# A two-layer decoder trunk: adaLN weights summed along rows on VectorE instead of multiplied on TensorE

## The chip, the cores and the metric

One NeuronCore of a Trainium2 chip runs the whole program. The metric is the device time of one execution in microseconds (us), as the median of several runs. TensorE is called PE in the rows (PEld is its weight load), VectorE DVE, ScalarE ACT, GpSimd POOL and SyncE SP.

## What is computed

Two layers work on x, which has 256 tokens of 2048 channels. The one vector c (2048 long) gives a shift, a scale and a gate for each channel of each layer:

```python
for li in range(DEPTH):                                   # DEPTH = 2
    mod = jax.nn.silu(c) @ w_ada[li] + b_ada[li]          # (2048) @ (2048, 6144)
    shift, scale, gate = jnp.split(mod, 3, axis=-1)
    h = rmsnorm(x, g_pre[li]) * (1.0 + scale) + shift
    p = split_columns(h @ w_in[li])                       # q, k, v, latents, indexer, gate columns
    ...                                                   # four token mixers A, B, C, D, 4 heads each
    mixed = concat(out_a, out_b, out_c, out_d) * silu(p["gate"])
    y = mixed @ w_out[li]
    x = x + gate * rmsnorm(y, g_post[li])
```

The line with `mod` is a matrix of 2048 by 6144 against a single vector, 50 MB of weights a layer that are each used once. The change is to this line alone. The large products (`w_in`, `w_out`) have 256 rows.

## The kernel before

**Large products.** Weights come as raw tiles of 128 x 1024 floats (512 KB, eight buffers called `raw`, DMAs issued by SP). ScalarE rounds each to `whi` (L279), VectorE subtracts to get `wlo` (L280), three buffers of each; then TensorE takes three products (`mm3`, L299 to L301: high by high, high by low, low by high). One raw tile is worth 24 products of 256 columns or 12 of 512. So each raw tile costs all three engines something, and each can run ahead of TensorE by as many tiles as there are buffers.

**Activations.** `modulated` (L433 to L436) scales x by `gain`, adds `shift` and splits the result into `act_hi` and `act_lo`. It needs the shift and gain of its 256 channels (one `k2` of eight), so it waits for their part of the adaLN product. `PHASES` says which k2 are taken together: layer 0 takes k2 0, then 1, then 2 and 3, and so on, layer 1 takes four at a time.

**adaLN.** The first two units of layer 0 (k2 0 and 1, `opening`) are 16 raw tiles that go through TensorE at once. The other 11 units, of 16 raw tiles each (layer 0: three of shift and scale, two of gate; layer 1: four and two), are a list of chunks that `Ada.run` hands out beside the large products: after every second raw tile `due` grows by a `PACE` of the stage, and for each whole 1 in it a chunk is issued. Most chunks are multiplied on VectorE by silu(c) (one value a partition, the input channel) and added to `ada_acc` (L131, L133). `PE_TILES` says how many of 16 go through TensorE instead (L141, `columns`: four products with 32 columns of weights each). At a unit's end `ada_acc` is summed over partitions by four more products with `ones` (L141), the result is in PSUM and is transposed (L162) into `shift` and `gain`, or gets bias and `g_post` (L182, L183) and goes to DRAM as `row` (L185), from where it is read back as a broadcast (L919). `until` issues what is left before a phase needs it; these all go through TensorE, as do five more at the start of layer 1 (`BOUND`).

**Order.** A scheduler orders each engine's instructions by priorities and its own estimate of time; engines take them strictly in that order. Between the layers the last tile of `w_out` is normed, x is updated (L960), squared and turned, and only then can layer 1 start.

## Time and profile before

| what | value |
|---|---|
| median of 3 runs | 1130.66 us (1130.19 to 1130.88) |
| the profiled execution | 1129.64 us |
| its span, first to last instruction | 1127.5 us |
| busy: TensorE | 1094.2 us, 97% |
| busy: VectorE | 848.9 us, 75% |
| busy: ScalarE | 553.9 us, 49% |
| read from HBM | 289.21 MB |

The span is what the rows below divide up; 2.1 us of the profiled execution lie around it. A share over the whole span mixes stages with different limits. In the span, 0 to 43 us is the opening, 43 to 60 the second phase's start, 60 to 490 the rest of layer 0 up to `w_out`, 490 to 571 `w_out` of layer 0, 571 to 592 the boundary, 592 to 900 the part of layer 1 that still has adaLN chunks, and 900 to 1127 the rest.

### The profile page before, as it was taken

The numbers are of one execution on the slowest core, as the hardware profiler recorded it, in microseconds if no ns is written. First come the engines' busy times: TensorE is split into PE (matmuls) and PEld (weight loads), VectorE is DVE, ScalarE is ACT, GpSimd is POOL, SyncE is SP. The second block draws the span as 40 slices with busy tenths as digits, with TensorE's granted clock in tenths as the row PEclk, the third lists the DMA queues.
The fourth block names the chain that finished last, engine by engine and source line by source line (L and its number), as shares of the span: only waits on it lengthen the run. The fifth ranks groups of instructions, "written<-read, shape, count | busy, mean of one in ns | idle before, by whom it ended". The sixth has DMA issues, their size and how long they took to land.

```text
span 1127.5 us, 19886 instructions
## 1 busy us (share of the span) xinstructions
PE 1094.2 (97%) x7818; PEld 991.5 (88%) x7818; DVE 848.9 (75%) x1221; ACT 553.9 (49%) x925; POOL 45.8 (4%) x57
## 2 busy tenths in 40 slices
PE   4899999999999999999989999999999999999996
PEld 3798989989899999988759999998899799999885
DVE  4587898889999978886549777899997555556454
ACT  3455344344464746754435445554644386645451
POOL 1000000000010100000000000100031000000000
PEclk9999999999999999999989999999999999999998
DMA  9997989868758888786869997977587654458642
GB/s 361 367 369 268 370 292 343 320 227 299 254 168 279 296 271 299 251 269 232 274 227 406 333 337 251 318 246 239 166 303 264 226 165 171 135 183 256 193 151 74
DMA packets 83101, 294.74 MB, mean 261 GB/s; under 512 B 9416, under 2 KB 9712, under 8 KB 83008
## 3 DMA queue, kind: packets, MB, share of 16 engines
q1 hardware_dynamic: 81216, 288.33, 73.5%
q0 software_dynamic: 1648, 5.09, 1.3%
q8 instruction: 61, 1.00, 0.4%
q14 instruction: 32, 0.26, 0.1%
q10 hardware_dynamic: 144, 0.07, 0.0%
HBM read 289.21 MB, written 4.23 MB: 260 GB/s over the span
## 4 chain that ended last, share of the span: by engine, by line
PE 89%; DVE 4%; DMA 3%; issue 1%; ACT 1%; SPq 0%; POOL 0%; DVEq 0%; POOLq 0%; ACTq 0%
PE main L299 26%; PE main L301 26%; PE main L300 26%; DMA raw<-in_w_ada_dram 3%; PE ada_ps L141 2%; DVE wlo L280 1%; PE att L491 1%; PE att L651 1%; PE att L508 1%; PE att L463 1%; DVE ada_acc L133 1%; DVE big L960 1%; ACT main L378 1%; PE att L616 0%; PE att L719 0%
## 5 line engine op out<-in xcount | busy, mean ns | idle before, releaser
L279 ACT CAST whi<-raw 128x1024 fp32r<-128x1024 f32 (+2 forms) x340 | 348.9, 1027 | 400.4 <-PE main L300 205.4
L280 DVE TENSOR_TENSOR wlo<-raw,whi 128x1024 fp32r<-128x1024 f32 (+2 forms) x340 | 404.7, 1195 | 155.4 <-ACT whi L279 153.8
L299 PE MATMUL main<-act_hi,whi 128*128 128x256 f32 x1568 | 440.0, 283 | 1.6 <-DVE lat_acc L369 1.6
L300 PE MATMUL main<-act_lo,whi 128*128 128x256 f32 x1568 | 441.0, 283 | 0.0
L301 PE MATMUL main<-act_hi,wlo 128*128 128x256 f32 x1568 | 433.1, 284 | 0.9 <-DVE wlo L280 0.8
L299 PEld LDWEIGHTS main<-act_hi,whi 128*128 128x128 f32 x1568 | 295.7, 189 | 5.7 <-issue 3.9
L300 PEld LDWEIGHTS main<-act_lo,whi 128*128 128x128 f32 x1568 | 295.6, 189 | 3.1 <-issue 2.0
L301 PEld LDWEIGHTS main<-act_hi,wlo 128*128 128x128 f32 x1568 | 290.7, 189 | 5.6 <-DVE wlo L280 2.3
L133 DVE SCALAR_TENSOR_TENSOR ada_acc<-raw,sc,ada_acc 128x1024 f32<-128x1024 f32 x144 | 184.7, 1282 | 35.8 <-DMA raw<-in_w_ada_dram 34.9
L300 PE MATMUL main<-wlo,act_hi 128*128 128x512 f32 (+2 forms) x552 | 209.3, 381 | 0.4 <-DVE wlo L280 0.3
L301 PE MATMUL main<-whi,act_lo 128*128 128x512 f32 (+2 forms) x552 | 206.7, 379 | 0.0
L299 PE MATMUL main<-whi,act_hi 128*128 128x512 f32 (+2 forms) x552 | 191.5, 381 | 4.8 <-ACT act_hi L435 4.8
L299 PEld LDWEIGHTS main<-whi,act_hi 128*128 128x128 f32 x552 | 103.3, 190 | 26.0 <-ACT act_hi L435 6.1
L300 PEld LDWEIGHTS main<-wlo,act_hi 128*128 128x128 f32 x552 | 104.5, 190 | 23.2 <-issue 2.7
L301 PEld LDWEIGHTS main<-whi,act_lo 128*128 128x128 f32 x552 | 104.4, 190 | 19.4
L141 PE MATMUL ada_ps<-raw,crep 128*32 128x128 f32 (+1 forms) x424 | 26.9, 381 | 12.8 <-DVE on L391 12.7
L100 POOL TENSOR_TENSOR rstd<-ms,mhalf 128x1 f32<-128x1 f32 (+1 forms) x12 | 8.9, 744 | 573.3 <-DVE ms L99 573.3
L141 PEld LDWEIGHTS ada_ps<-raw,crep 128*32 128x32 f32 x424 | 13.9, 131 | 20.5 <-DVE on L391 12.7
L455 ACT ACTIVATE lat_acc<-lat_acc,mx 128x256 f32<-128x256 f32 (+1 forms) x56 | 25.2, 452 | 8.9 <-DVE mx L453 8.9
L949 ACT ACTIVATE wk<-main 128x512 f32<-128x512 f32 x16 | 9.5, 594 | 31.4 <-PE main L301 31.4
L659 DVE SCALAR_TENSOR_TENSOR cbuf<-wk,wid,cbuf 128x128 f32<-128x128 f32 (+1 forms) x64 | 24.2, 412 | 0.1
L656 ACT ACTIVATE wk<-att 128x256 f32<-128x256 f32 (+1 forms) x32 | 15.2, 488 | 18.2 <-DVE cbuf L659 13.0
(201 smaller groups left out, 873.5 us busy)
## 6 DMA issues: line engine op xcount, KB each, us to landing
raw<-in_w_g_dram SPq DMA_DIRECT2D x240, 512.0 KB, 5.4
raw<-in_w_ada_dram SPq DMA_DIRECT2D x192, 512.0 KB, 5.4
raw<-in_w_out_dram SPq DMA_DIRECT2D x64, 512.0 KB, 4.6
raw<-in_w_g_dram SPq DMA_DIRECT2D x16, 400.0 KB, 5.9
raw<-in_w_g_dram SPq DMA_DIRECT2D x16, 384.0 KB, 4.1
raw<-in_w_uq_dram SPq DMA_DIRECT2D x6, 384.0 KB, 4.0
big<-in_xt_dram SPq DMA_DIRECT2D x4, 512.0 KB, 6.8
raw<-in_w_ukv_dram SPq DMA_DIRECT2D x4, 512.0 KB, 4.4
```

Source lines behind the costliest of these rows:

```text
L133: nc.vector.scalar_tensor_tensor(self.acc, w, sc[:, kt:kt + 1], self.acc, op0=ALU.mult, op1=ALU.add)
L141: nc.tensor.matmul(self.ps[32 * q:32 * q + 32, 0:n], lhs, w[:, n * q:n * (q + 1)], start=not self.started, stop=last, tile_position=(0, 32 ...
L279: nc.scalar.copy(hi, src)
L280: nc.vector.tensor_sub(lo, src, hi)
L299: nc.tensor.matmul(out, sh, mh, start=first, stop=False, **kw)
L300: nc.tensor.matmul(out, sh, ml, start=False, stop=False, **kw)
L301: nc.tensor.matmul(out, sl, mh, start=False, stop=last, **kw)
L378: nc.scalar.activation(jk, L.cols(t, 512 * h, 512), AF.Square, accum_out=ssp[:, h:h + 1])
L455: nc.scalar.activation(lg[:, i, :], lg[:, i, :], AF.Exp, bias=mx[:, i:i + 1], accum_out=sm[:, i:i + 1])
L463: nc.tensor.transpose(tp[:, b * P:(b + 1) * P], pr[:, b * P:(b + 1) * P], ident)
L656: nc.scalar.activation(rl[:, 0:2 * sw], dp[:, 0:2 * sw], AF.Relu)
L659: nc.vector.scalar_tensor_tensor(sc[t], rl[:, u * sw:(u + 1) * sw], wid[:, t, h:h + 1], sc[t], op0=ALU.mult, op1=ALU.add)
```

## The change

The chunks after the opening units are laid out the other way around: output channels on partitions, input channels along the row. A unit is now one k2 (256 channels of shift and of scale) or four columns of gates, with 8 chunks, so the number of raw tiles stays 176 beside the opening's 16. Each chunk is one VectorE instruction: the tile times 0.5 times a row of silu(c), summed along the row into one column of `part`. `make_row` fills that row for all partitions: a broadcast DMA of c (1 MB written to `scb`, on POOL's queue), four tanh on ScalarE and four instructions of 512 columns on VectorE. A unit ends with one addition of its parts and the two or three small instructions of 2 to 4 columns that the bias needs; L141 remains for the opening alone. The gate is now written to DRAM from a tile of 128 x 8 as 1024 single floats. The biases and `g_post` come with the small constants, so four DMAs of 256 KB go away. To make room, `crep` takes the place of `strip`, and the tile `on` has one buffer instead of two. Paces change, `PE_TILES` and `BOUND` go.

```diff
-PACE = {"phase1": 1.5, "phase": 1.7, "last": 1.25, "gate0": 0.25, "gate1": 1.75, "gate2": 1.75, "gate3": 1.5, "d": 1.0, "out": 0.5, "next": 1}
+PACE = {"open": 0, "phase1": 1.75, "phase": 1.7, "last": 1.25, "gate0": 0.5, "gate1": 1.75, "gate2": 1.75, "gate3": 1.75, "d": 1.0, "out": 1.0, "next": 1}
-PE_TILES = {"phase1": 0, "phase": 2, "last": 2, "gate0": 1, "gate1": 1, "gate2": 0, "gate3": 0, "d": 0, "out": 2, "next": 0}
-UPTO = [[None, None, (0, 1), (0, 2), (0, 3)], [None, (1, 3)]]
+UPTO = [[None, None, (0, 3), (0, 5), (0, 7)], [None, (1, 7)]]
...
+    scb = const.tile([P, D], F32, name="scb")
+    def make_row():
+        row = a["c_row"]
+        nc.gpsimd.dma_start(scb, bass.AP(tensor=row.tensor, offset=row.offset, ap=[[0, P], [1, D]]))
+        for q in range(4):
+            v = scb[:, 512 * q:512 * (q + 1)]
+            th = work.tile([P, 512], F32, name="wk")
+            nc.scalar.activation(th, v, AF.Tanh, scale=0.5)
+            nc.vector.scalar_tensor_tensor(v, th, 1.0, v, op0=ALU.add, op1=ALU.mult)
...
-            if on_pe:
-                self.columns(crep[:, kt, :], w, last and self.acc is None)
-            elif self.acc is None:
-                self.acc = lay.tile([P, 1024], F32, name="ada_acc")
-                with tc.issue_after(self.behind):
-                    nc.vector.tensor_scalar(self.acc, w, sc[:, kt:kt + 1], None, op0=ALU.mult)
-            else:
-                nc.vector.scalar_tensor_tensor(self.acc, w, sc[:, kt:kt + 1], self.acc, op0=ALU.mult, op1=ALU.add)
-            if last:
-                if self.acc is not None:
-                    self.columns(ones[:, 0:32], self.acc, True)
+            with tc.issue_after(self.behind):
+                nc.vector.scalar_tensor_tensor(w, w, 0.5, scb[:, 1024 * (n % 2):1024 * (n % 2 + 1)],
+                                               op0=ALU.mult, op1=ALU.mult, accum_out=self.part[:, n:n + 1])
+            if n == 7:
                 self.finish(layers[li], li, u)
...
         def finish(self, L, li, u):
+            v = small.tile([P, 4], F32, name="parts")
+            nc.vector.tensor_add(v, self.part[:, 0:8:2], self.part[:, 1:8:2])
+            if u < K2:
+                self.modulation(L, u, v[:, 0:2], v[:, 2:4])
...
+                gc = self.gate[:, 4 * j:4 * j + 4]
+                nc.vector.tensor_add(gc, v, L.par[:, c0:c0 + 4])
+                nc.vector.tensor_mul(gc, gc, L.par[:, c0 + 16:c0 + 20])
+                if j == 1:
+                    L.row[h] = row = dram.tile([8, P], F32, name=f"row{li}{h}")
+                    nc.gpsimd.dma_start(bass.AP(tensor=row.tensor, offset=row.offset, ap=[[1, P], [P, 8]]), self.gate)
...
         if li == 1:
-            ada.until(1, 1)
-            ada.step(BOUND, on_pe=True)
+            ada.until(1, 3)
```

On TensorE, in layer 0's second phase, before. The rows with `ada_ps` are adaLN (a chunk, then the sum over partitions with `ones`), the others `w_in` products:

```order
L299 MATMUL main<-whi,act_hi_278 128x512 x2
L141 MATMUL ada_ps<-raw,crep 32x256 x4
L141 MATMUL ada_ps<-ada_acc,ones 32x256 x2
L300 MATMUL main<-wlo,act_hi_278 128x512
L301 MATMUL main<-whi,act_lo_282 128x512
```

The same place now:

```order
L304 MATMUL main<-whi,act_hi_278 128x512 x2
L305 MATMUL main<-wlo,act_hi_278 128x512
L306 MATMUL main<-whi,act_lo_282 128x512
```

All such rows after the opening are gone from TensorE; nothing takes their place.

On VectorE, at the start of the second phase (about 43 us), before. `sml` are the small constants, `big_96` is x:

```order
L162 STREAM_TRANSPOSE wk<-ada_ps 128x128
L168 TENSOR_TENSOR shift<-wk,sml 128x2
L170 SCALAR_TENSOR_TENSOR gain<-wk,sml 128x2
L172 TENSOR_TENSOR gain<-gain,sml 128x2
L433 SCALAR_TENSOR_TENSOR wk<-big_96,gain,rrow 128x256 x2
L280 TENSOR_TENSOR wlo<-raw,whi 128x768
L436 SCALAR_TENSOR_TENSOR act_lo_282<-wk,shift,act_hi_278 128x256 x2
L131 TENSOR_SCALAR ada_acc<-raw,sc 128x1024
L133 SCALAR_TENSOR_TENSOR ada_acc<-raw,sc,ada_acc 128x1024 x2
L280 TENSOR_TENSOR wlo<-raw,whi 128x1024
```

The same place now:

```order
L161 STREAM_TRANSPOSE wk<-ada_ps 128x128
L118 SCALAR_TENSOR_TENSOR scb<-wk,scb 128x512
L171 TENSOR_TENSOR shift<-wk,sml 128x2
L173 SCALAR_TENSOR_TENSOR gain<-wk,sml 128x2
L118 SCALAR_TENSOR_TENSOR scb<-wk,scb 128x512
L175 TENSOR_TENSOR gain<-gain,sml 128x2
L118 SCALAR_TENSOR_TENSOR scb<-wk,scb 128x512
L438 SCALAR_TENSOR_TENSOR wk<-big_96,gain,rrow 128x256 x2
L285 TENSOR_TENSOR wlo<-raw,whi 128x768
L118 SCALAR_TENSOR_TENSOR scb<-wk,scb 128x512
L441 SCALAR_TENSOR_TENSOR act_lo_282<-wk,shift,act_hi_278 128x256 x2
L137 SCALAR_TENSOR_TENSOR raw,part<-raw,scb 128x1024 x3
```

Four instructions of `make_row` stand between the opening's last transpose and the first adaLN chunk.

On VectorE at the start of layer 1 (about 587 us), before; `att` holds x turned:

```order
L433 SCALAR_TENSOR_TENSOR wk<-att,gain,rrow 128x256 x6
L280 TENSOR_TENSOR wlo<-raw,whi 128x800
L436 SCALAR_TENSOR_TENSOR act_lo_6428<-wk,shift,act_hi_6424 128x256
L280 TENSOR_TENSOR wlo<-raw,whi 128x800
L436 SCALAR_TENSOR_TENSOR act_lo_6428<-wk,shift,act_hi_6424 128x256 x3
L131 TENSOR_SCALAR ada_acc<-raw,sc 128x1024
L436 SCALAR_TENSOR_TENSOR act_lo_6429<-wk,shift,act_hi_6425 128x256 x2
L433 SCALAR_TENSOR_TENSOR wk<-att,gain,rrow 128x256 x2
L280 TENSOR_TENSOR wlo<-raw,whi 128x768
```

The same place now:

```order
L438 SCALAR_TENSOR_TENSOR wk<-att,gain,rrow 128x256 x6
L441 SCALAR_TENSOR_TENSOR act_lo_6377<-wk,shift,act_hi_6373 128x256 x3
L438 SCALAR_TENSOR_TENSOR wk<-att,gain,rrow 128x256 x2
L441 SCALAR_TENSOR_TENSOR act_lo_6377<-wk,shift,act_hi_6373 128x256
L137 SCALAR_TENSOR_TENSOR raw,part<-raw,scb 128x1024 x3
L441 SCALAR_TENSOR_TENSOR act_lo_6378<-wk,shift,act_hi_6374 128x256 x4
L137 SCALAR_TENSOR_TENSOR raw,part<-raw,scb 128x1024 x2
L285 TENSOR_TENSOR wlo<-raw,whi 128x768
L285 TENSOR_TENSOR wlo<-raw,whi 128x800
```

The first three subtractions of layer 1 (800, 800 and 768 columns) have moved ahead of the boundary, behind those of `w_out`; five chunks now stand ahead of the fourth.

## Rows read from the trace of the kernel before

**Rows 1.** Page, chain that ended last, share of the span by engine

```profile
PE 89%; DVE 4%; DMA 3%; issue 1%; ACT 1%; SPq 0%; POOL 0%; DVEq 0%; POOLq 0%; ACTq 0%
```

**Rows 2.** Stretches: length, us of PE, PEld, DVE, ACT, POOL; clock; DMA share, GB/s

```profile
4.00:14.00 10.00, 1.17 (x20) 0.74 (x24) 5.63 (x14) 4.57 (x10) 0.00 (x0) 1.00 1.01 397
...
43.00:60.00 17.00, 13.31 (x90) 12.38 (x90) 16.82 (x26) 6.14 (x7) 0.57 (x1) 0.90 0.98 375
60.00:490.00 430.00, 429.30 (x3211) 397.30 (x3208) 377.20 (x550) 217.73 (x376) 18.50 (x22) 1.00 0.82 286
245.00:365.00 120.00, 120.00 (x900) 110.50 (x899) 114.79 (x205) 59.65 (x108) 5.99 (x9) 1.00 0.77 258
490.00:571.00 81.00, 81.00 (x361) 63.65 (x360) 46.07 (x44) 33.54 (x43) 0.00 (x0) 1.00 0.74 248
...
592.00:900.00 308.00, 307.94 (x2255) 286.50 (x2254) 254.06 (x374) 152.40 (x241) 18.00 (x15) 1.00 0.80 282
```

**Rows 3.** Waits, 60 to 490 us: waiter, releaser: total us, times, longest

```profile
DVE wlo L280 <- ACT whi L279: 29.8, 33, 2.5
DVE ada_acc L133 <- DMA raw<-in_w_ada_dram: 9.7, 6, 2.0
...
PE main L301 <- DVE wlo L280: 0.7, 2, 0.5
```

**Rows 4.** Stretches, line 141 alone: PE busy, PEld busy, clock, DMA

```profile
60.00:490.00 430.00, 9.79 (x100) 2.60 (x96) 1.00 0.82 286
490.00:571.00 81.00, 1.91 (x20) 0.46 (x20) 1.00 0.74 248
571.00:592.00 21.00, 8.97 (x100) 3.75 (x100) 0.85 0.73 254
592.00:900.00 308.00, 4.40 (x32) 1.02 (x32) 1.00 0.80 282
```

**Rows 5.** Timeline of PE around one adaLN sum: start, us, instruction

```profile
94.58 0.40 PE L301 MATMUL main<-whi,act_lo 128*128 128x512 f32 x1
94.91 0.63 PE L141 MATMUL ada_ps<-ada_acc,ones 128*32 128x256 f32 x4
95.46 0.73 PE L299 MATMUL main<-whi,act_hi 128*128 128x512 f32 x2
96.03 0.40 PE L300 MATMUL main<-wlo,act_hi 128*128 128x512 f32 x1
```

**Rows 6.** Groups by line: count, busy us, mean ns of one, idle before

```profile
L133 DVE SCALAR_TENSOR_TENSOR ada_acc<-raw,sc,ada_acc 128x1024 f32<-128x1024 f32 x144 | 184.7, 1282 | 35.8 <-DMA raw<-in_w_ada_dram 34.9
L455 ACT ACTIVATION_READ_ACCUMULATOR lat_acc<-lat_acc,mx 128x1 f32 x56 | 10.5, 187 | 0.0
L391 DVE TENSOR_TENSOR on<-on,wk 128x512 f32<-128x512 f32 x7 | 4.8, 691 | 1.3 <-ACT wk L389 0.9
L172 DVE TENSOR_TENSOR gain<-gain,sml 128x4 f32<-128x4 f32 (+1 forms) x9 | 1.4, 159 | 0.2
```

**Rows 7.** Stretches, tile ada_acc alone: PE, PEld and DVE busy

```profile
60.00:490.00 430.00, 5.62 (x48) 1.53 (x48) 105.42 (x85) 1.00 0.82 286
...
592.00:900.00 308.00, 4.40 (x32) 1.02 (x32) 73.85 (x59) 1.00 0.80 282
```

**Rows 8.** Timeline of the boundary, PE and DVE

```profile
587.08 4.50 PE L141 MATMUL ada_ps<-raw,crep 128*32 128x256 f32 x40
587.48 2.44 DVE L433 SCALAR_TENSOR_TENSOR wk<-att,gain,rrow 128x256 f32<-128x256 f32 x6 [0.42 <-ACT rrow L411]
591.50 1.02 PE L299 MATMUL main<-whi,act_hi 128*128 128x400 f32 x2
592.04 1.27 DVE L436 SCALAR_TENSOR_TENSOR act_lo<-wk,shift,act_hi 128x256 fp32r<-128x256 f32 x3
599.37 0.95 DVE L280 TENSOR_TENSOR wlo<-raw,whi 128x768 fp32r<-128x768 f32 x1
```

**Rows 9.** Page, DMA issues: count, KB each, median us to landing

```profile
strip<-line POOLq DMA_DIRECT2D x1, 1536.0 KB, 14.0
```

More of the change, by code (lines that the diff above doesn't have):

```diff
@@ L60 @@
 OWN3 = 1
-SM_PAR, SM_LAM, SM_END = 16, 128, 640
+UNITS_OF = 12
+SM_PAR, SM_LAM, SM_END = 16, 196, 708
+N_PAR = 90
 @with_exitstack
@@ L103, in trunk @@
     sc = const.tile([P, KT], F32, name="sc")
-    crep = const.tile([P, KT, 32], F32, name="crep")
+    crep = lay.tile([P, 12 * S], F32, name="strip")[:, 0:32 * KT].rearrange("p (k r) -> p k r", r=32)
     nc.scalar.activation(sc, c_sb, AF.Tanh, scale=0.5)
@@ L171, in to_columns @@
                                            op0=ALU.add, op1=ALU.add)
[L172 removed]
+            nc.vector.tensor_mul(g, g, L.par[:, 32 + 2 * k2:34 + 2 * k2])
         def finish(self, L, li, u):
[L175 to L185 removed]
+            v = small.tile([P, 4], F32, name="parts")
@@ L187, in stage @@
         def stage(self, name, unit):
-            self.pace, self.pe, self.unit = PACE[name], PE_TILES[name], unit
+            self.pace, self.unit = PACE[name], unit
         def add(self, li, u):
-            self.todo += [(li, u, n) for n in range(KT)]
+            self.todo += [(li, u, n) for n in range(8)]
         def run(self, pace):
@@ L196, in run @@
                 self.due -= 1
-                self.step(on_pe=(self.todo[0][2] + 1) * self.pe % 16 < self.pe)
+                self.chunk(*self.todo.pop(0))
         def until(self, li, u):
             while self.todo and self.todo[0][:2] <= (li, u):
-                self.step(on_pe=True)
+                self.chunk(*self.todo.pop(0))
             self.due = 0.0
-        def step(self, n=1, on_pe=False):
-            for _ in range(n):
-                if self.todo:
-                    self.chunk(*self.todo.pop(0), on_pe)
     ada = Ada()
@@ L248, in load_small @@
             nc.vector.tensor_scalar(L.gsub[:, j:j + 1], L.par[:, 53:54], (1.0 - lam_init) / (1 + j), None, op0=ALU.mult)
-    strip = const.tile([P, 12, S], F32, name="strip")
+    strip = None
     def make_strip():
+        nonlocal strip
+        strip = lay.tile([P, 12, S], F32, name="strip")
         hot = work.tile([P, 512], F32, name="wk")[0:32, 0:384]
@@ L383, in norm_rows_of_turned @@
     def norm_rows_of_turned(L):
-        acc = work.tile([P, 2, S], F32, name="on", bufs=2)
+        acc = work.tile([P, 2, S], F32, name="on", bufs=1)
         for k2 in range(K2):
@@ L694, in branch_d @@
         for t in range(T):
-            on = work.tile([P, 512], F32, name="on", bufs=2)
+            on = work.tile([P, 512], F32, name="on", bufs=1)
             ssq = small.tile([P, 4], F32, name="dss")
@@ L829, in layer @@
             if li == 0 and n < 2:
-                ada.stage("out", 0)
-                ada.pace = 0 if n == 0 else PACE["phase"]
-                ada.pe = PE_TILES["phase"]
+                ada.stage("phase" if n else "open", 0)
             else:
                 ada.stage(("last", "next")[li] if end else ("phase", "phase1")[li], UNIT["early"] if end and li == 0 else 0)
-            ada.limit = upto or (1, 5)
+            ada.limit = upto or (1, UNITS_OF)
             if li == 1 and n == 0:
@@ L861, in layer @@
                             next(units)
+                make_row()
                 continue
@@ L975, in trunk @@
     ada.pace = 0
-    for u in range(1, 4):
+    for u in range(2, K2):
         ada.add(0, u)
@@ L979, in trunk @@
         if li == 0:
-            for l, u in ((0, 4), (0, 5), *((1, u) for u in range(6))):
+            for l, u in (*((0, u) for u in range(K2, UNITS_OF)), *((1, u) for u in range(UNITS_OF))):
                 ada.add(l, u)
```

69 lines of the change are left out of this document (28 added, 41 removed).

## The prediction, made before the changed kernel was run

> **What bounds the kernel now.** I read the chain that ended last first: 89% of it is TensorE [rows 1]. Then the stretches [rows 2]: from 60 to 490 us TensorE is busy in 429.3 of 430 us, in `w_out` and in layer 1 all the time. So what leaves TensorE there is gained, unless another engine becomes late. VectorE is the only candidate: 377.2 of 430 us in layer 0, 114.79 of 120 (95.7%) between 245 and 365 us, and still no stall of TensorE there. Third, who waits [rows 3]: between 60 and 490 us TensorE waits 0.7 us for VectorE. VectorE's own largest wait, 29.8 us, is for ScalarE's `whi`, which comes late because its three buffers are full: real slack. Another 9.7 us are waits for the adaLN tiles themselves, which are no use to anyone. The kernel is bound by TensorE, with VectorE close behind it in layer 0.
>
> **What TensorE loses.** The rows of line 141 [rows 4] are its adaLN work: 9.79 us from 60 to 490, 1.91 in `w_out`, 8.97 at the boundary, 4.40 in layer 1. Busy time is not the price, since a switch of tile costs something on both sides. In the timeline [rows 5] a `ones` sum of two products of 0.63 us stands between main products that otherwise follow each other by 0.23 us (in `w_out` of 512 columns the same). From the start of L301 at 94.58 to that of L300 at 96.03 are 1.45 us, for three main products (0.69): the sum costs 0.76 us, 1.2 times its busy time. So 11.8 us go in layer 0, 2.3 in `w_out`, 5.3 in layer 1. The boundary I take below.
>
> **What VectorE gets.** The old multiply-add, with two float tiles read from SBUF, takes 1.282 us [rows 6]; the new one has the same size and two such inputs, so this is its price before the summing output. VectorE has no instruction of that kind in this kernel. ScalarE has: each of its summing instructions shows a second row that reads the sum, 0.187 us [rows 6]. I call this extra r, per chunk: 0 at one end (it may be hidden under the next start), 0.19 at the other; I take 0.1, the middle, since VectorE's own small instructions are shorter (0.159 us for four columns [rows 6], which overlap).
>
> The Trainium skill, page "VectorE: DVE Perf Modes", section "Two Vector instructions with no wait between them", says that an instruction that also writes out its accumulator is two instructions, the main one and an accumulator read. No run of before shows that on VectorE; the ScalarE row agrees in kind. By that rule r is above 0: at 0.19 the sum is that of rival 2 below, while at 0 it would be some 4 us under the forecast.
>
> In layer 0 from 60 us to `w_out` the new order has, by count, 97 chunks (105 up to the first `w_out` evacuation, less 8 in the second phase's start): 97 x 1.282 = 124.4 us for the 105.42 of before [rows 7]; 48 small instructions instead of 12, 36 x 0.159 = 5.7. Transposes and bias additions that go (some 3.5 us) offset the rest of the small stuff in part; I take them off: 377.2 + 19.0 + 5.7 - 3.5 = 398.4 us, and 97r on top: 398 to 417, 408 at r = 0.1. TensorE needs 430 - 11.8 = 418.2. So VectorE would be at 95.3% of the new length with r = 0, just what 245 to 365 us bears without a stall, at 97.6% with 0.1 and at 99.7% with 0.19. An engine that takes instructions in order, with waits for tiles between them, doesn't reach 100%. With 0.1 the length lies between TensorE's need, 418, and VectorE's work at that 95.7%, 408 / 0.957 = 426: I take 422.5, a gain of **7.5 us** instead of 11.8 (bounds 12 and a loss of 5).
>
> **The opening** pays for `make_row`. Its DMA writes 1 MB, stands third on POOL's queue and so runs with x and the first weights, where DMA is full at 397 GB/s (the 4 to 14 us row [rows 2]): 1.05 MB / 397 = **2.6 us** (bounds 0, if the opening waits for something else, and 2.6). Then, from 43 to 60 us, VectorE is busy 16.82 of 17 us while TensorE has gaps [rows 2]: here VectorE is the bound. The new order puts four instructions of 512 columns there, 4 x 0.69 = 2.8 us [rows 6], ahead of the first chunk; the first chunk of a unit was a cheaper form (some 0.5 us), and r counts six times (0.6): **3.9 us** (bounds 2.5, as the four tanh and part of this may fall into waits, and 6.5, as two more chunks come before the tenth split). ScalarE's four tanh lie beside it; its 6.14 of 17 us hide them. TensorE is full from 60 us on, so this delay stays to the end.
>
> **`w_out` and the rest of layer 0.** The pace there doubles, five chunks more: 46.07 + 5 x 1.4 = 53 of 79 us, hidden. The gain is 2.3 us.
>
> **The boundary.** At 587.08 us TensorE still has 4.50 us of adaLN work, and the first product of layer 1 follows at 591.50 [rows 8]. Nothing of it is left, and the first two splits lie ahead of the boundary, so that product could start some 1.5 us earlier. But VectorE's order now is: six scalings (2.44 us from 587.48), three `act_lo` (1.27), two scalings and one `act_lo` (1.2), three chunks (3.8), four `act_lo` (1.7), two chunks (2.6), and only then the fourth split: its start at 600.5 us against 599.37 for the fourth before [rows 8]. TensorE has three tiles' work for that time, 12 products of at most 0.23 us each [rows 5], 8 us, and runs out. I take **+1 us** (bounds -2 and +4). The granted clock of this stretch is 0.85 on average [rows 4], a mix of its two levels; I count neither loss nor gain of clock.
>
> **Layer 1, 592 to 900 us.** 62 chunks for 73.85 us of multiply-adds [rows 7]: 79.5, small instructions 3, less transposes: 254.06 + 5.6 + 6 = 266 of 303 us, 88%. TensorE's 5.3 us are gained but for 1 us of stalls where VectorE is dense (the attention stages): **4.3**.
>
> **At nothing.** The gate's row is written as 1024 single floats from POOL. The nearest row is `strip`, 1536 pieces in 14.0 us [rows 9]. Behind the last gate product some 27 (layer 0) and 47 (layer 1) splits of about 1.2 us stand in VectorE's order before the row is used, 30 us and more; without that cover it would cost some 15 us per layer. The four DMAs of 256 KB that go were off the path. `on` with one buffer makes ScalarE wait for four transposes between two halves of branch D; ScalarE is busy 217.7 of 430 us [rows 2], so nothing (up to 1 us a layer without that slack). `crep` in `strip`'s place is free long before `strip` is filled.
>
> **The sum.** +2.6 + 3.9 - 7.5 - 2.3 + 1.0 - 4.3 = -6.6 us against the profiled execution's 1129.64 (span 1127.5 and 2.14 around it): 1123.0. That execution lies 1.0 us under the median, so **1124 us** as a median, and 1117 to 1130 by the smaller bounds.
>
> **Rivals.**
> 1. *All of it is gained*: r near 0 and no stalls. +2.6 + 3.3 - 11.8 - 2.3 - 1.0 - 5.3 = -14.5: 1116 us (1110 to 1117). For it: 245 to 365 us runs at 95.7% without stalls, and the new paces put chunks where VectorE was idle. Against it: in-order waits and any r.
> 2. *VectorE becomes the bound of layer 0*: r = 0.19, 417 us of work at the 95.7%: 435.5 for the 430 of before, +5.5. With +2.6 + 4.4 for the opening, -1.5, +2.5 for the boundary (five chunks are 1 us longer) and -2.5: +11, 1142 us; 1131 to 1142 by how dense VectorE can run. It decides from r of about 0.11 (at 95.7%) to 0.19 (at 97.5%): there layer 0 gives less than the opening takes. For it: VectorE's 16.82 of 17 us at 43 to 60 with gaps on TensorE. Against it: TensorE's mere 0.7 us of waiting now.
> 3. *The change doesn't do what it says*, because another stall takes the place of the old work, so that the time stays: within 0.2%. The order shows the products gone, so this is only a balance of the terms above, 1130 us.
>
> **How the numbers follow.** Forecast 0.47, rival 1 0.23, rival 2 0.22, rival 3 0.08. A measurement of this kernel can tell about 0.2% (2.3 us) from no change: 1128.4 to 1132.9. Of the forecast's own range nearly all lies under 1128.4 (0.39), rival 1 wholly (0.23): faster 0.62. Same: 0.07 + 0.04 + 0.07 = 0.18; slower 0.20. The range reaches into rival 1 and half of rival 2: 1112 to 1137 leaves out about 1 in 10 at the top and some 0.07 below.
>
> **What would show it.** Line 141's successor has no TensorE row after 43 us. The new chunk's rows show 1.28 us, and whether a second row stands behind each: this decides between the rivals. TensorE's waits on VectorE between 60 and 490 us: under 1 us in rival 1, some 4 us here, over 15 in rival 2. Layer 0's `w_out` starts some 1 us earlier than now in my sum (6.5 lost, 7.5 gained). The first full stretch of TensorE starts 5 to 7 us later than 56 to 60. I'd be wrong if the opening hides the 1 MB, if the boundary stalls more than 4 us, or if DMA waits of chunks spread on the fuller VectorE.

## The result, and the profile after

The changed kernel takes **1179.79 us** (median of 4 runs, 1175.63 to 1181.93); the kernel before, beside it, 1130.77 (1130.19 to 1131.22). The ratio is 1.0429, 95% interval 1.0399 to 1.0459. It is slower by 49 us; the prediction said 1124 and at most 1137. The profiled execution has a span of 1180.2 us against 1127.5.

The page of the kernel after: the span, the busy times and the chain that ended last, to be held against [rows 1].

```profile
span 1180.2 us, 19623 instructions
...
PE 1098.7 (93%) x7562; PEld 1009.3 (86%) x7562; DVE 872.0 (74%) x1466; ACT 557.2 (47%) x929; POOL 38.7 (3%) x54
...
PE 67%; DMA 15%; DVE 12%; issue 3%; ACT 1%; SPq 0%; POOL 0%; DVEq 0%; POOLq 0%
```

TensorE's share of the chain falls from 89% to 67%; a load (DMA, 15%) and VectorE (12%) take its place. Over the span VectorE is no fuller than it was (74%, before 75%; 872 us of work, before 849): it is late, not overloaded. The groups by line show the new instruction, to be held against the first of [rows 6] (columns as there):

```profile
L137 DVE SCALAR_TENSOR_TENSOR raw<-raw,scb 128x1024 f32<-128x1024 f32 x176 | 214.3, 1223 | 99.8 <-DMA raw<-in_w_ada_dram 99.4
...
L137 DVE DVE_READ_ACCUMULATOR raw<-raw,scb 128x1 f32 x176 | 14.6, 83 | 0.0
```

A second row does stand behind each instruction, 83 ns long, but the instruction that follows starts together with it (both at 339.04 in the timeline below). So it takes no time of its own: where VectorE does not wait, 1.144 us pass from the start of a tile's instruction to the start of the next one (median of 162), and 1.197 us did for the old multiply-add (127). What is worse than before is the last number of the first row: VectorE stands still for 99.4 us in front of these instructions because the tile has not landed; before it was 34.9.

Who waits from 60 to 490 us, the stretch of [rows 3]:

```profile
DVE raw L137 <- DMA raw<-in_w_ada_dram: 41.1, 26, 8.0
...
PE main L306 <- DVE wlo L285: 16.9, 9, 6.1
...
DVE wlo L285 <- ACT whi L284: 15.1, 23, 1.6
```

VectorE's waits for tiles are up from 9.7 to 41.1 us, and TensorE's for VectorE's splits from 0.7 to 16.9. VectorE's slack, its wait for `whi`, is down by half. SyncE's queue, which issues every load, waits too (L294 is the main weights' load, L135 the adaLN tiles'; whole span):

```profile
SPq L294 <- DVE raw L137: 177.4, 84, 9.9
SPq L135 <- DVE raw L137: 96.1, 64, 4.0
```

That is 274 us of waiting until VectorE's instruction on an adaLN tile gives a buffer back; the kernel before has 71.0 and 47.8, 119 us, at the same place (there 144 of the tiles' instructions are multiply-adds on VectorE, here all 176). This closes a ring: the load waits for a buffer, the buffer for VectorE, VectorE for the load.

**Where the time goes.** The main products of both kernels come in the same order, so one can be held against the other: the lag of the k-th product is its start in one trace less its start in the trace of the kernel before. I give it at the time that the product has in the kernel before. The names are those of the experiments below.

| time before, us | after | row_turned | both | before_all_vector | before_floats | after_inorder | inorder_d0 |
|---|---|---|---|---|---|---|---|
| 54 | 5.9 | 5.7 | 5.8 | 0.9 | 0.2 | 6.6 | 6.0 |
| 249 | -0.4 | 0.1 | 0.1 | -2.7 | 1.0 | -0.3 | -0.9 |
| 346 | 10.5 | 3.4 | 2.7 | 0.5 | 1.0 | -1.0 | -1.6 |
| 400 | 17.6 | 12.6 | 11.8 | 0.0 | 11.2 | -0.2 | -0.8 |
| 424 | 24.0 | 11.8 | 11.4 | 0.0 | 20.1 | 6.8 | 0.0 |
| 502 | 34.6 | 19.6 | 20.7 | 0.5 | 18.7 | 2.8 | -2.6 |
| 559 | 41.1 | 24.4 | 23.1 | 2.9 | 18.7 | 2.4 | -2.8 |
| 602 | 40.2 | 23.5 | 21.4 | 6.3 | 18.5 | 1.7 | -3.4 |
| 866 | 52.3 | 28.2 | 19.5 | 6.0 | 30.7 | 2.8 | -2.6 |
| 1115 | 52.6 | 29.6 | 19.7 | 6.0 | 30.9 | 2.9 | -2.5 |

The column "after" says: the opening costs 6 us; from 54 to 249 us the change gives 6.3 back, as a gain was forecast for this stretch (7.5 for all of 60 to 490); then 41.5 us are lost between 249 and 559, and 12 more between 602 and 866. These two stretches hold what has to be explained.

The largest single wait shows what happens. VectorE's timeline of the kernel after (start, us, engine, line; in brackets the idle time ahead and what ended it), and below it SyncE's queue at that time:

```profile
329.56 0.27 DVE L675 MATCH_REPLACE8 cbuf<-m,cbuf 128x128 f32<-128x128 f32 x1
337.88 1.22 DVE L137 SCALAR_TENSOR_TENSOR raw<-raw,scb 128x1024 f32<-128x1024 f32 x1 [8.05 <-DMA raw<-in_w_ada_dram]
339.04 0.08 DVE L137 DVE_READ_ACCUMULATOR raw<-raw,scb 128x1 f32 x1
339.04 1.22 DVE L285 TENSOR_TENSOR wlo<-raw,whi 128x1024 fp32r<-128x1024 f32 x1
```

```profile
322.70 2.52 SPq L294 DMA_DIRECT2D raw<-in_w_g_dram  x2
326.88 0.33 SPq L135 DMA_DIRECT2D raw<-in_w_ada_dram  x1
328.81 10.66 SPq L294 DMA_DIRECT2D raw<-in_w_g_dram  x2
```

The load is issued at 326.88 and VectorE is at its instruction 3 us later. The split at 339.04, which TensorE waits for, stands behind it. Two things are wrong here: the load has a start of only 3 us, and it takes 11 where the median of these loads is 5.2. The stretch in which it lies (length; us of PE, PEld, DVE, ACT, POOL; clock; DMA share, GB/s):

```profile
325.00:350.00 25.00, 18.95 (x144) 18.75 (x143) 16.05 (x44) 12.21 (x27) 0.00 (x0) 0.86 0.73 175
```

TensorE loses 6 us here, and its granted clock falls to 0.86 on average: some of the products behind the stall run at the lower of the two levels. So this wait costs more than its length.

### The profile page after: what moved, and what is told of

Read it like the earlier page. It is cut to its first block, busy times and chain, and to the rows that moved or that the text cites. A ratio compares the mean times of both kernels' runs of the same rounds, so it can differ in the third digit from the quotient of the medians.

```text
span 1180.2 us, 19623 instructions
## 1 busy us (share of the span) xinstructions
PE 1098.7 (93%) x7562; PEld 1009.3 (86%) x7562; DVE 872.0 (74%) x1466; ACT 557.2 (47%) x929; POOL 38.7 (3%) x54
## 4 chain that ended last, share of the span: by engine, by line
PE 67%; DMA 15%; DVE 12%; issue 3%; ACT 1%; SPq 0%; POOL 0%; DVEq 0%; POOLq 0%
PE main L306 21%; PE main L305 21%; PE main L304 20%; DMA raw<-in_w_ada_dram 11%; DVE wlo L285 4%; DVE raw L137 3%; DMA raw<-in_w_g_dram 3%; DMA raw<-in_w_out_dram 2%; PE att L656 1%; PE att L496 1%; PE att L513 1%; PE att L468 1%; DVE big L961 1%; ACT whi L284 1%; ACT main L383 0%
## 5 line engine op out<-in xcount | busy, mean ns | idle before, releaser
L306 PE MATMUL main<-act_hi,wlo 128*128 128x256 f32 x1568 | 440.0, 288 | 20.6 <-DVE wlo L285 20.4
L304 PE MATMUL main<-act_hi,whi 128*128 128x256 f32 x1568 | 446.1, 287 | 3.7 <-DVE lat_acc L374 3.7
L305 PE MATMUL main<-act_lo,whi 128*128 128x256 f32 x1568 | 445.8, 286 | 0.0
L306 PEld LDWEIGHTS main<-act_hi,wlo 128*128 128x128 f32 x1568 | 294.9, 191 | 26.3 <-DVE wlo L285 23.8
L305 PEld LDWEIGHTS main<-act_lo,whi 128*128 128x128 f32 x1568 | 298.8, 191 | 1.4 <-issue 0.3
L137 DVE SCALAR_TENSOR_TENSOR raw<-raw,scb 128x1024 f32<-128x1024 f32 x176 | 214.3, 1223 | 99.8 <-DMA raw<-in_w_ada_dram 99.4
L305 PE MATMUL main<-wlo,act_hi 128*128 128x512 f32 (+2 forms) x552 | 212.7, 387 | 7.3 <-DVE wlo L285 7.2
L306 PEld LDWEIGHTS main<-whi,act_lo 128*128 128x128 f32 x552 | 105.5, 192 | 23.5 <-DVE act_lo L913 4.6
L144 PE MATMUL ada_ps<-raw,strip 128*32 128x128 f32 x256 | 11.5, 340 | 14.2 <-DMA raw<-in_w_ada_dram 14.1
L449 ACT ACTIVATE lat_acc<-lat_acc,rc 128x128 f32<-128x128 f32 (+1 forms) x48 | 18.4, 444 | 10.4 <-DVE rc L488 10.4
L144 PEld LDWEIGHTS ada_ps<-raw,strip 128*32 128x32 f32 x256 | 8.7, 136 | 15.6 <-DVE on L396 14.1
```

Source lines behind the costliest of these rows:

```text
L137: nc.vector.scalar_tensor_tensor(w, w, 0.5, scb[:, 1024 * (n % 2):1024 * (n % 2 + 1)], op0=ALU.mult, op1=ALU.mult, accum_out=self.part[:, ...
L144: nc.tensor.matmul(self.ps[32 * q:32 * q + 32, 0:n], lhs, w[:, n * q:n * (q + 1)], start=not self.started, stop=last, tile_position=(0, 32 ...
L304: nc.tensor.matmul(out, sh, mh, start=first, stop=False, **kw)
L305: nc.tensor.matmul(out, sh, ml, start=False, stop=False, **kw)
L306: nc.tensor.matmul(out, sl, mh, start=False, stop=last, **kw)
L449: nc.scalar.activation(out, src, AF.Copy, scale=by)
```

## The experiments

All times are medians, and each ratio is against runs of the kernel before on the same chip (medians 1129.9 to 1130.7). Two theories stood at the start of the experiments. **A**: the gate's row, written in 1024 single floats, chokes the DMA engines. **B**: the new paces put too many tiles where VectorE has no time. A third, **C**, says that both act through VectorE's in-order wait for tiles.

### Row write, paces, and the wait itself

**row_turned**: the 128x8 columns are turned on TensorE and written as eight runs of 512 bytes.

```
-  nc.gpsimd.dma_start(bass.AP(tensor=row.tensor, offset=row.offset, ap=[[1, P], [P, 8]]), self.gate)
+  tp = psd.tile([P, 512], F32, name="ada_ps")[0:8, 0:P]
+  nc.tensor.transpose(tp, self.gate, ident)
+  tr = work.tile([P, 512], F32, name="wk")[0:8, 0:P]
+  nc.scalar.copy(tr, tp)
+  nc.gpsimd.dma_start(row, tr)
```

> Only the gate's row write is changed: the 128x8 columns are turned on TensorE into 8x128 and written as eight runs of 512 bytes instead of 1024 single floats; all else as in the kernel after. Theory A (the single floats choke the DMA engines): in the kernel after, the 4 KB weight packets fall from 80-100 per us to 5-20 per us for about 9 us behind each of the four row writes (320, 414, 832, 940 us). TensorE's lag against the kernel before grows there by about 8 (325-366), 6 (400-441) and 11 us (797-866). Without the choke these go: about 1155 us, and no stretch of 9 us with under 20 packets per us. Theory B (too many chunks at the wrong places, whatever the row write): 1175-1180 us, the lag at the same places as in the kernel after.

Measured: 1158.98 us, ratio 1.0259 (1.0244 to 1.0274), 21 us less than the kernel after. The lag no longer jumps at 346 us (3.4, was 10.5). The DMA issues (KB each, median us from issue to landing) of the row write, first in the kernel after, then here:

```profile
row<-gcol POOLq DMA_DIRECT2D x4, 4.0 KB, 11.2
```

```profile
row<-wk POOLq DMA_DIRECT2D x4, 4.0 KB, 4.7
```

A holds for 21 of the 49 us as the kernel after stands.

**old_paces** (`phase1` 1.5, `gate0` 0.25, `gate3` 1.5, `out` 0.5, as before) and **both** (these paces and the turned row).

> The kernel after with the paces of the kernel before (phase1 1.5 not 1.75, gate0 0.25 not 0.5, gate3 1.5 not 1.75, out 0.5 not 1.0). Theory B (chunks placed more densely block VectorE's in-order queue behind tiles that have not landed): the 18 us of lag that arise between 477 and 560 us and some of those in the gates go, about 1158 us. Theory A (the row writes cost it): 1175-1180 us.

> Row write turned and the paces of the kernel before. If A and B add, 1179.8 - 25 - 20 = about 1135 us, within 1% of the kernel before. If either alone holds the whole loss, this is no better than that one alone. If the loss sits in the in-order wait for tiles itself, wherever they are placed, it stays above 1150 us.

Measured: 1170.84 us (ratio 1.0355, 1.0324 to 1.0386) and 1149.59 us (1.018, 1.0164 to 1.0196). The paces are worth 9 us, not the 20 or so that were expected, and the two add: 21 + 9 = 30. But with both undone some 20 us remain, though tiles, paces and row writes now stand much as before. Neither A nor B is the whole.

**resident**: the instruction reads the resident row twice instead of the loaded tile.

```
-  scalar_tensor_tensor(w, w, 0.5, scb[...], ...)
+  scalar_tensor_tensor(f, f, 0.1, f, ...)       # f = scb[...]
```

> The kernel after, but each chunk's VectorE instruction reads the resident row twice instead of the tile just loaded (the tile is still loaded, on the same queue, into the same eight buffers); the product with the adaLN weights is left out. Theory C (VectorE's in-order wait for tiles that have not landed, 99.4 us in 58 waits, and the buffers held meanwhile, are the way by which A and B reach TensorE): VectorE's waits for these tiles are gone, its load is unchanged at about 870 us, and the time falls to about 1120-1125 us in spite of row writes and paces. If VectorE's load itself were too much (the prediction's second rival), it stays above 1165 us. If the slow DMA reaches TensorE through its own weight tiles instead, it lies near 1150 us.

Measured: 1199.72 us, ratio 1.0616 (1.056 to 1.0672). VectorE's waits for these tiles are gone, and yet it is the slowest of all. SyncE's queue shows why (L295 is the main weights' load):

```profile
SPq L295 <- DMA raw<-in_w_ada_dram: 496.2, 120, 14.5
```

With nobody reading the tile, its buffer is handed on at once, and the queue waits for the adaLN load that it has just issued before it may load main weights over it. The run put a new wait in the old one's place and decides nothing on C.

### The form, the buffers, the opening

**before_all_vector**: the kernel before with `PE_TILES` at zero everywhere. **D** says that these 20 us come from sending every tile through VectorE.

> The kernel before with its share of adaLN tiles for TensorE set to zero in every stage (but for the eight and five tiles at the layer boundary): the tiles' order, paces, layout, accumulating form and row write stay as they were. Theory D (what is lost in layer 0 beyond row writes and paces comes from sending every tile through VectorE, in order, so that it waits for each tile to land and TensorE waits behind it): about 1140 us, that is 10 us and more above the kernel before, with VectorE's waits for adaLN tiles well above 34.9 us. The prediction's own step (TensorE is relieved and the waits on VectorE are of no use to anyone): about 1123-1126 us. Theory E (it is the new layout's row write by TensorE, the resident row and the shared buffers that cost it): 1128-1132 us.

Measured: 1134.99 us, ratio 1.004 (1.0025 to 1.0055). Layer 0 up to 502 us shows a lag of 0.5: moving these tiles from TensorE to VectorE gains nothing there in the old form, but it costs nothing either (the 5 us are lost later, between 502 and 602). D falls.

This run gives something to compare with. For the adaLN tiles 41 to 89 in order of loading (issued at 187 to 424 us) I took from each trace the time from the load's issue to the moment when VectorE gets to the instruction (its start less the idle time ahead of it):

| kernel | median start of the load, us | under 5.5 us | VectorE's waits for these 49 tiles, us |
|---|---|---|---|
| before_all_vector | 8.1 | 12% | 3.8 |
| after | 5.4 | 51% | 34.1 |
| both | 5.5 | 51% | 23.4 |
| both_lag | 5.3 | 53% | 19.9 |
| both_raw9 | 5.7 | 43% | 14.3 |
| after_inorder (below) | 13.4 | 0% | 0.0 |

A load takes 5.2 us (median in the kernel after). In the new form 45% of the tiles are asked for sooner than that (`after` and `both` alike; before_all_vector 8%). Counted in the order of instructions, 4.1 splits whose weights were loaded *before* the tile stand behind the tile's instruction on VectorE (mean of these 49 in `both`, and the same in the kernel after); in before_all_vector it is 2.4 (after_inorder, below: none). The change put the tiles further forward in VectorE's row. Why it did so is open: the old instructions hang on each other through `ada_acc` and the new ones do not, but no run tried that. Call this **G**: not more work for VectorE, but an order in which a tile is asked for too early.

**both_lag**: each tile's product is written one tile after its load.

> Row write turned and paces of before, and each tile's VectorE instruction one tile later than its load (the load of tile n is issued, then the product of tile n-1). Theory D: VectorE's waits for adaLN tiles fall from 65.1 us (row write turned and old paces) to under 25 us, the 20 us of lag between 264 and 502 us go by half or more, about 1138 us. If the buffers bind instead (a tile that lies one step longer in one of eight shared buffers holds up the load of the main weights), waits on main weights rise and the time stays at 1150 or above.

Measured: 1147.37 us, 1.0151 (1.0128 to 1.0175); waits 64.9 us, as before (65.1). The place in the text is not the place in the row: the count of splits behind the tile is 4.1 here too, number by number as in `both`. So this does not speak against G; it did not move the order.

**both_raw9**: silu(c)'s row in bf16, a ninth buffer, the row made from two of the buffers.

> Row write turned and paces of before, silu(c)'s row kept in bf16 (4 KB less per partition) and the room spent on a ninth buffer for loaded tiles. If the eight shared buffers bind (the queue that issues all loads waits for a buffer that a tile not yet multiplied holds), loads start earlier, VectorE's waits for adaLN tiles fall from 65.1 us by a third or more: about 1140 us. If lateness comes from elsewhere: 1148-1150 us.

Measured: 1143.06 us, 1.0112 (1.0085 to 1.0139). The lag at 502 us falls from 20.7 to 2.9, but 10 us are lost between 602 and 866. The leads are hardly longer (5.7). The run changes the opening and the second operand's type as well, so I don't put its 6.5 us down to the buffer alone.

**both_late_row**: silu(c)'s row from the 16 columns, turned and broadcast behind the opening.

> Row write turned and paces of before, and silu(c)'s row no longer made by a 1 MB load at the start and eight instructions of ScalarE and VectorE behind the opening: the 16 columns of silu(c) that exist anyway are turned on TensorE, written as 16 runs of 512 bytes and broadcast by a 1 MB load behind the opening's loads. Theory F (the opening's loss of 5.8 us at 54 us is the load's 2.3 and the eight instructions' 3.5): the lag at 54 us falls to 1-2 us and the time to about 1145 us. If the 5.8 us come from the opening's tiles themselves: 1149 us.

Measured: 1152.2 us, 1.0196 (1.0172 to 1.0219), no gain. The lag at 58 us is -1.7, at 79 us 7.5: the first tiles wait for the row instead. The opening's cost was moved.

### The order alone

**both_inorder** (on `both`) and **after_inorder** (on the kernel after): one line. Each tile's instruction is queued on VectorE behind the split traced last, so that the buffers are emptied in the order in which they were filled.

```
-        nc.vector.tensor_sub(lo, src, hi)
+        ada.behind = nc.vector.tensor_sub(lo, src, hi).ins
```

> Row write turned, paces of before, and one order more: on VectorE each adaLN tile's instruction is queued behind the split traced last, so that tiles leave the shared buffers in the order in which they were loaded. Theory G (the new form stands too early in VectorE's row: between 195 and 425 us VectorE reaches a tile 5.5 us (median) after its load was issued, against 8.1 us in the kernel before with all tiles on VectorE, and a load takes 5.4 us): VectorE's waits for adaLN tiles fall from 65.1 to under 15 us, the lag no longer grows between 264 and 502 us, time 1128-1136 us (opening +6 stays). If VectorE's load or the buffers bind: 1145 us and more, with waits on main weights.

> The kernel after with that order alone; row writes in single floats and the new paces stay. Theory G alone holds the loss: about 1135 us. The row writes act by themselves too (theory A: main weights, too, come late while the DMA engines are choked): about 1150 us. The order is nothing: 1180 us.

Measured: 1135.14 us (1.0045, 1.0031 to 1.0059) and **1133.96 us** (1.0029, 1.0017 to 1.0041). The one line takes 46 of the 49 us away, with the single floats and the new paces still there. The scheduler makes every order anew, but SyncE's 564 DMAs of after_inorder follow each other, tensor by tensor, as in the kernel after but for 17 places. Counted as above, no split of earlier loaded weights is left behind any of the 49 tiles. The group of the new instruction in after_inorder has no idle time ahead of it any more, where the kernel after has 99.8 us:

```profile
L137 DVE SCALAR_TENSOR_TENSOR raw<-raw,scb 128x1024 f32<-128x1024 f32 x176 | 212.5, 1224 | 0.0
```

and SyncE's waits for the buffers that this instruction frees are down from 274 to 104 us:

```profile
SPq L294 <- DVE raw L137: 60.9, 76, 2.1
SPq L135 <- DVE raw L137: 42.9, 53, 3.0
```

The loads now wait for the splits instead (546 us, in the kernel after 428), so the queue does not wait much less; what it waits for is no longer an engine that waits for a load. Turning the row and undoing the paces add nothing to it (1135.1 against 1134.0). So G is the cause of the loss, and A and B make it worse: in the new form a choke or a denser pace does harm only while tiles have no lead.

**before_floats**: the kernel before, its row written in 1024 floats 16 bytes apart, the columns permuted to match.

```
-  nc.gpsimd.dma_start(L.row[h], sb[0:P:32, 0:256])
+  row = L.row[h]
+  nc.gpsimd.dma_start(bass.AP(tensor=row.tensor, offset=row.offset, ap=[[1, 4], [4, 256]]), sb[0:P:32, 0:256])
```

> The kernel before with the gate's row written in 1024 single floats 16 bytes apart (the columns are permuted to match), nothing else changed. Theory A: the weight packets fall to 5-20 per us for about 9 us behind each of four row writes here too; the kernel before has its loads further ahead, so between 8 and 25 us are lost: 1138-1155 us. If the choke only costs where VectorE waits for the tile at hand: 1131-1134 us.

Measured: 1156.87 us, 1.0236 (1.021 to 1.0262): 26.7 us, in three jumps of the lag (10 up to 400, 9 up to 424, 12 up to 866). The row's landing, to be held against 4.3 us in the kernel before:

```profile
row<-wk POOLq DMA_DIRECT2D x4, 4.0 KB, 20.2
```

So the choke is real by itself, and the kernel before does not bear it. In the first and the third jump VectorE waits for one adaLN tile (11.2 and 15.0 us), and TensorE 6.6 and 10.9 us for the split behind it. In the second it is a tile of the main weights that comes late: ScalarE waits 9.0 us for it and TensorE 6.5, so that one does not go by the adaLN tiles. This write is also a longer choke than that of the kernel after (landing 20.2 us against 11.2). after_inorder bears the write of the kernel after. The weight packets (4 KB) that start per us behind the write's issue, from the DMA records of the traces:

| write | first 14 us behind its issue |
|---|---|
| before, 340.6 | 60 71 31 54 45 59 100 99 100 104 73 83 53 52 |
| after, 320.6 | 5 0 0 57 52 5 0 10 7 6 5 9 16 55 |
| after_inorder, 340.8 | 97 72 68 10 0 4 10 9 9 8 10 9 73 94 |

The third row shows nine microseconds at a tenth of the rate, as in the second, and after_inorder loses nothing there (lag 0.1 at 331, -1.6 at 358 us).

**both_inorder_stage**: the opening's row made from two of the eight buffers, fp32.

> As the run with row write turned, paces of before and the order, and silu(c)'s row (fp32) made from two buffers of the shared eight, so that its 1 MB load waits for a buffer instead of leaving at the start. Theory F: the lag at 58 us falls from 6.8 to about 2 us, so 4-5 us less than the run without it: 1124-1131 us.

Measured: 1137.47 us, 1.0054 (1.0034 to 1.0074). The lag at 79 us is 2.9 instead of 5.0, but the time is not better; inconclusive.

### What the order leaves

In after_inorder the lag falls from 5.8 at 79 us to -1.6 at 358, then jumps to 6.8 at 424.

> The kernel after with the order behind the last split for tiles traced inside a weight product, and none for the tiles that the attention stages trace. If the 7 us at 400-425 come from eight tiles in one piece behind one split: the lag there stays under 2 us, 1127-1130 us. If the freed tiles come too early again and VectorE waits for them: 1134-1142 us, with waits for adaLN tiles above 5 us.

> The kernel after with each tile behind the last split but one. The tiles lie one split shorter in the buffers (lead about 10-11 us instead of 13.4, still well above the 5.4 us of a load): waits for adaLN tiles stay near 0; if a tile's hold on a buffer costs time, some us less than 1134; if not, 1134.

> As after_inorder_free, with silu(c)'s row made from two of the shared buffers. If the opening's lag falls by 2-3 us as it did with the order before, 2-3 us less than after_inorder_free: 1124-1128 us, the first version below both kernels.

Measured: after_inorder_free 1139.42 us (1.0087, 1.0071 to 1.0102), after_inorder_two 1143.76 (1.0122, 1.0107 to 1.0137), stage_free 1139.17 (1.0082, 1.0067 to 1.0096). All are worse than after_inorder, the lag at 424 us is as high in each of them (7.1, 7.0, 6.4), and after_inorder_two loses 14 us more between 480 and 488. A loosened order is not a cure.

**before_inorder**: the kernel before with the order on its VectorE tiles.

> The kernel before with the same order on its tiles for VectorE. If it carries a part of the fault (34.9 us of VectorE's waits for adaLN tiles): waits near 0 and 1125-1129 us. If its leads were long enough: 1130 us. If the longer hold on the buffers costs it: 1132-1136 us.

Measured: 1132.83 us, 1.0023 (1.0012 to 1.0034). The kernel before didn't need it and loses 2.6 us. The order is a need of the new form, no gain in itself.

**inorder_d0**. SyncE's queue in after_inorder, and the stretches (columns as above):

```profile
398.07 18.81 SPq L135 DMA_DIRECT2D raw<-in_w_ada_dram  x8
417.70 0.33 SPq L294 DMA_DIRECT2D raw<-in_w_g_dram  x1
```

```profile
410.00:415.00 5.00, 5.00 (x37) 4.74 (x35) 3.17 (x8) 4.34 (x17) 0.57 (x1) 1.00 0.69 64
...
420.00:425.00 5.00, 3.80 (x33) 3.59 (x31) 5.00 (x10) 0.38 (x1) 0.00 (x0) 1.00 1.02 392
425.00:430.00 5.00, 3.41 (x14) 2.91 (x14) 4.30 (x7) 4.77 (x10) 0.00 (x0) 0.66 1.03 418
```

Eight adaLN loads in one piece fill the eight buffers, and the weights of the next product are issued behind them, at 417.70. The 64 GB/s at 410 us are another thing, the choke of the second row write (issued at 402.2; the DMA engines are at 69%). They are not what costs the 7 us: both_inorder, with its row turned, jumps as well (lag -1.6 at 400, 6.0 at 424 us), and inorder_d0 has the choke without the jump. Six of the eight tiles are traced by branch D's attention. The edit, on top of the one line of after_inorder:

```
-PACE = {... "gate0": 0.5, ...}
-UNIT = {... "d": 2}
+PACE = {... "gate0": 1.5, ...}
+UNIT = {... "d": 0}
```

> The kernel after with the order, and the six tiles that branch d's attention traced in one piece with two others traced with the gate of that branch instead (none at the attention, gate0's pace 1.5 for 0.5). If the piece of eight loads costs the 7 us at 400-425: the lag stays near -1 us there, and the time falls from 1134 to 1126-1129 us. If they are lost to something else at that place: 1133-1136 us.

> The same with silu(c)'s row made from two of the shared buffers. If the opening's 2-3 us come through to the end: 1123-1127 us; if later stages take them back, as in the run with the order and paces of before: as inorder_d0.

Measured: **1126.04 us** (1124.88 to 1127.05), ratio 0.9959 (0.9945 to 0.9972), and 1126.53 us (0.9966, 0.9953 to 0.9979). The lag at 424 us is 0.0, and at the end -2.5, though the row write (issued at 401.6) chokes the DMA engines there too:

```profile
410.00:415.00 5.00, 5.00 (x39) 4.79 (x37) 3.40 (x9) 4.34 (x16) 0.95 (x2) 1.00 0.63 83
```

This is a version of the change that beats the kernel before, by 0.4%. Whether the kernel before would gain from the same piece being taken apart was not tried; in its trace TensorE has no stall there [rows 2]. The second run, with the row made from two buffers, has no shorter opening (lag 5.7 at 79 us, against 5.2), so it does not test what that would be worth.

From 60 to 490 us of inorder_d0, to be held against the third line of [rows 2], and below it the tiles' instructions (L137) alone, on VectorE:

```profile
60.00:490.00 430.00, 430.00 (x3168) 406.08 (x3168) 392.28 (x684) 222.40 (x380) 15.86 (x19) 1.00 0.83 289
...
60.00:490.00 430.00, 112.23 (x186) 1.00 0.83 289
```

TensorE has no gap, VectorE is at 91%. Of the 186 rows 93 are tiles and 93 their accumulator reads.

## Why the prediction was wrong, point by point

**The step that failed** is in its first paragraph: VectorE's 9.7 us of waits for tiles "are no use to anyone", and so were left out of the sum. The last line of its list of dangers named the case ("if DMA waits of chunks spread on the fuller VectorE"), but gave it no place, no price and no chance of its own. It was wrong in kind, too: the waits did not come from a fuller VectorE. The order of the kernel after, which was there to be read, has the tiles' instructions 4.1 splits ahead of where their loads stand (mean of the 49 above); no step compared an instruction's place in VectorE's row with its load's place in SyncE's. after_inorder shows that this is the cause: 46 of 49 us go when these places are made the same. The prediction's sign for rival 2, TensorE waiting over 15 us for VectorE between 60 and 490 us, came true with 16.9, but it can't tell a late VectorE from an overloaded one.

**"At nothing": the gate's row write.** It asked how long the write itself takes and what covers that (30 us and more, right). It did not ask what the write does to the loads beside it. In the kernel after it is worth 21 us, a like write in the kernel before 26.7 us, and nothing once the tiles have a lead of 13 us. The Trainium skill, page "DMA: Bandwidth & Descriptors", section "Rules for kernel authors", says that a strided, non-contiguous last dimension becomes one descriptor per element. The landing of 11.2 us for 4 KB, against 4.7 for eight runs, fits that; the trace has the write as 16 packets of 256 bytes and shows no descriptors. That the traffic beside it drops to a tenth, the packet rows show.

**r, the price of the chunk.** Forecast 1.282 + 0.1, r between 0 and 0.19. Measured are 1.223 and a read of 0.083 that runs beside the next instruction; by the starts the new instruction is 0.053 us cheaper than the old, so r lies below its lower bound. Rival 2 decided from r of 0.11, and that condition is not met: the 1180 lies far beyond its 1142 for another reason. The Trainium skill, page "VectorE: DVE Perf Modes", section "Two Vector instructions with no wait between them", has an instruction with an accumulator output as two; the 176 second rows agree. That r is above 0 by that rule, as the prediction had it, they do not bear out.

**The opening** was forecast at +2.6 + 3.9 = 6.5 us; the lag at 54 us is 5.9. The two parts are right as well: the first product of `w_in` starts at 27.06 us instead of 24.98 (2.1), and the other 3.8 come by 54 us. No run had it back at the end: both_late_row and both_inorder_stage moved it or lost it later, and both_raw9 (lag 0.7 at 54 us) changes other things too.

**Layer 0.** Forecast -7.5 us for 60 to 490. In the kernel after, 6.3 of it are there by 249 us and then buried. In inorder_d0 the lag goes from 6.0 at 54 us to -2.6 at 502: -8.6 us. The size is right once nothing waits, but that is luck. The forecast kept 4.3 of TensorE's 11.8 us back because VectorE would be too full, with 408 us of work. It has 392: the tiles take 112 us (93 of them), not 134 (97 at 1.382). TensorE waits for nothing in this stretch; what keeps the gain down is the next point.

**A term that nobody had: longer main products.** From start to start, the main products of 256 columns that follow each other take 119.8 to 119.9 ns in all 16 traces of the new form, and 117.9 to 118.3 in the four of the old form. Summed product by product over the lag's steps of at most 12 ns, inorder_d0 loses 3.8 us by it from 54 to 502 us and 5.1 from 602 to the end; before_all_vector loses 0.1 and nothing. Without it layer 0 would give 12.4 us, about all of TensorE's 11.8. Why products of the same shape are longer in the new form stays open: no run tried it.

**`w_out`, boundary, layer 1.** Forecast -2.3, +1.0, -4.3. In the kernel after +6.5 (502 to 559 us), -0.9 (559 to 602), +12.4 (602 to the end). In inorder_d0 -0.2, -0.6 and +0.9. The boundary came out slightly better than forecast. In `w_out` of inorder_d0 some 2 us of products are gone, and two waits for a split, which the forecast called hidden, take them back (490 to 571 us; the kernel before has none):

```profile
PE main L305 <- DVE wlo L285: 1.8, 2, 0.9
```

The 4.3 us of layer 1 are there: -4.2 but for the 5.1 of the longer products.

**The sum.** In inorder_d0 the parts as measured, 6.0 - 8.6 - 0.2 - 0.6 + 0.9, give -2.5 us at the last product, and 1126.0 as a median, near the 1124 of the forecast. So the forecast priced the change with its order mended and the piece of eight loads taken apart, not the change as it stood. That it comes so near is luck in part: without the longer products the same parts would give -11.4 us, with them they give -2.5, and the forecast of -6.6 had neither.

## What to carry to other kernels

When work moves to an in-order engine, its busy share is half of the question; the other half is how long before the engine gets to an instruction its load was issued, and what stands behind that instruction in the row. Count it from the orders of the two queues before trusting a sum of busy times. Where loads share a pool of buffers, try first to have them consumed in the order in which they were issued; here that was worth 46 us in the new form and lost 2.6 in the old. A scattered write is priced by what it does to the loads beside it, not by its own landing.

## What the runs showed of the hardware

- 1024 writes of 4 bytes (512 bytes apart) bring the weight packets from 50 to 100 per us down to under 20 for nine us, and raise the mean time of a 4 KB packet from 0.21 us (in the 20 us before the first write of the kernel after) to 0.72 us (in the nine behind it). The write's own 16 packets take 0.49 us at most. With four partitions as the source and 16 bytes between the floats the landing is 20.2 us.
- VectorE's read of an accumulator takes 83 ns and starts as the next instruction does. The product with summing output is 59 ns shorter than the multiply-add with a tile as third operand (1.223 against 1.282 us for 1024 columns), and the next instruction starts 1.144 us after it, against 1.197.
- Main products of the same 256 columns follow each other 1.5 to 2 ns later in every trace of the new form than in those of the old; over 5052 of them that is some 9 us. The cause is not known.
- A stall can cost TensorE more than its length. In `both`, where layer 0's `w_out` begins (columns as above):

```profile
496.00:500.00 4.00, 0.21 (x3) 0.01 (x1) 3.69 (x6) 2.79 (x8) 0.00 (x0) 0.97 0.37 137
500.00:506.00 6.00, 4.60 (x10) 3.20 (x11) 4.96 (x11) 0.86 (x3) 1.38 (x1) 0.50 0.68 211
506.00:512.00 6.00, 6.00 (x28) 4.81 (x28) 2.29 (x2) 2.69 (x3) 0.00 (x0) 0.95 0.46 149
```

  After 3.8 us without work the granted clock is 0.50, the 1.2 GHz level, for 6 us: ten products, where 1.4 of the 6 us are a second wait; in the 6 us after it, nearly at full clock, there are 28. The lag grows by 9 us between 476 and 502 us of the kernel before, over stalls of 5.2.
